# Gate and up products of a SwiGLU layer by seven block products instead of eight, with the down projection between them

## The chip, the cores and the metric

The kernel runs on one core of a Trainium2 chip. The metric is the device time of one execution in microseconds (us); lower is better. Engines are named as in the profile: PE is TensorE (PEld its weight loads), DVE VectorE, ACT ScalarE, POOL GpSimd, SP SyncE, whose queue issues the transfers.

## What is computed

A trunk of two layers on 512 tokens of width 1024: each layer is an attention (stick-breaking in the first, dilated windows in the second), then a SwiGLU of width 2816, each after an RMS norm and added to the residual stream; a last norm gives the output. All data is float32. The part that matters here:

```python
def _rmsnorm(h, g):
    hf = h.astype(jnp.float32)
    y = hf * lax.rsqrt(jnp.mean(hf * hf, axis=-1, keepdims=True) + NORM_EPS)
    return (y * g.astype(jnp.float32)).astype(h.dtype)

def _swiglu(h, w_gate, w_up, w_down):
    return (jax.nn.silu(h @ w_gate) * (h @ w_up)) @ w_down

    h = h + _swiglu(_rmsnorm(h, norm_ffn[layer]), w_gate[layer], w_up[layer], w_down[layer])
```

## The kernel before

**Data.** The residual stream H lies transposed on chip: 8 chunks of 128 model columns on the partitions, 512 tokens along the free dimension. A float32 product is made from float32r operands in three matmuls: each operand is split into a high part (rounded by a copy on ScalarE) and a low part (the difference, by VectorE), and high x high, high x low and low x high are added up in PSUM (`mm3`, L290). X holds both parts of the normed stream without its factor 1/rms; that factor, a row R of 512 tokens, is applied to the products.

**Weights.** The class `Weights` (L150) streams them in the order of their use as units of 128 x 512. `load` (L175) issues one transfer on SP's queue into one of 8 raw buffers; `split` (L186) makes the high part `whi` on ScalarE (L214) and the low part `wlo` on VectorE (L215); `get` (L220) hands out a unit and has those up to three units ahead split.

**Feed-forward layer** (`ffn`, L739). 22 chunks of 128 hidden columns. For a chunk, `gu` (L743) fills two PSUM banks, gate and up, with 8 x 3 matmuls of 512 columns each, from two weight units per bank; then VectorE scales the gate by R (L758), ScalarE applies SiLU (L759), GpSimd multiplies by R again (L762), VectorE multiplies by the up bank (L763), and the result is split into VO (L767, L768). `down` (L771) multiplies a part of the chunks (PARTS: 6, 6, 6 and 4 chunks) by the down weights for each of 8 output columns and adds the bank to H (`residual`, L651). `ffn_order` (L43) puts each part two chunks behind its last `gu`. `rstd_row` (L366) makes R from the sums of squares while chunk 0 is computed. In layer 1 the last part is `finish` (L798): it goes over the first half of the tokens for all outputs and then over the second, so that half the output can be normed and stored beside the other's products; its matmuls have 256 columns, and its weights stay on chip (`khi`, `klo`).

**Order.** The code writes instructions in the order of the lists above. The framework that builds the program then sets each engine's queue itself: it tracks which buffer each instruction reads and writes, adds the waits, and may put an instruction that is ready ahead of an earlier one that is not. Within a queue the instructions then start in that order. PSUM has 8 banks: three `z`, two `t`, two `pj`, one `av`.

```python
 23  PARTS = [(0, 6), (6, 12), (12, 18), (18, 22)]
290      def mm3(out, wh, wl, xh, xl, start, stop):
291          mm(out, wh, xh, start, False)
292          mm(out, wh, xl, False, False)
293          mm(out, wl, xh, False, stop)
651      def residual(n, p, e=slice(0, 512)):
652          dve.tensor_add(H[:, n, e], H[:, n, e], p[:, e])
```

Of the kernel before, what the change touches and what calls it, by code (L numbers as in the profile page):

```python
# [7 lines left out]
F = mybir.dt.float32  # L8
# [23 lines left out]
# Chunks of the output per transfer, and those that GpSimd scales, for both halves of the tokens.  # L32
# [9 lines left out]

def ffn_order():  # L43
    seq = []
    done = 0
    for i, (a, b) in enumerate(PARTS):
        upto = min(b + 2, NF) if i + 1 < len(PARTS) else NF
        for f in range(done, upto):
            seq.append(("gu", f))
        done = upto  # L50
        seq.append(("dn", i))
# [9 lines left out]
def raw_list():  # L61
    """Weight tiles in the order of their use: each holds two units."""
    raws = []
    for layer in range(2):
        raws += [(kind, layer, i) for kind, i in mixer_order()]
        for kind, i in ffn_order():
            if kind == "gu":
                raws.append(("gu", layer, i))
            else:
                raws += [("dn", layer, i, n) for n in range(0, 8, 2)]  # L70
    return raws


def raw_width(r):
    if r[0] == "dn":
        a, b = PARTS[r[2]]
        return 2 * 128 * (b - a)
    return 2048


def pack_weights(w_qkv_a, w_o_a, w_kv, w_q_b, w_o_b, w_gate, w_up, w_down):
    """The weights in the order of their use, each tile in the layout that it has on chip."""
# [4 lines left out]
    def block(m, r):  # L87
        return m[:, 256 * r[2]:256 * r[2] + 256].reshape(8, 128, 256).transpose(1, 0, 2).reshape(128, -1)
# [6 lines left out]
    for r in raw_list():  # L95
        l = r[1]
        if r[0] == "qk":
            t = cross(r, [cols(wq[l], r[2]), cols(wk[l], r[2])])
        elif r[0] == "v":
            t = [block(wv[l], r)]  # L100
        elif r[0] == "o":
            b = [block(wo[l], (0, 0, g)) for g in range(4)]
            t = [b[g][:, 512 * q:512 * q + 512] for g, q in O_ORDER[4 * r[2]:4 * r[2] + 4]]
        elif r[0] == "gu":
            t = cross(r, [cols(w_gate[l], r[2]), cols(w_up[l], r[2])])
        else:
            a, b = PARTS[r[2]]
            m = w_down[l][128 * a:128 * b]
            t = cross(r, [cols(m, r[3]), cols(m, r[3] + 1)])
        parts.append(np.concatenate(t, axis=1).reshape(-1))  # L110
# [3 lines left out]
def held(r):  # L114
    """The last part of the last layer's weights stays on chip for both halves of the tokens."""
    return r[0] == "dn" and r[1] == 1 and r[2] == len(PARTS) - 1


def crossed(r):
    """Whether the two units of a tile are used half by half in turn."""  # L120
    return r[0] in ("qk", "gu") and r[2] == 0 or (
        r[0] == "dn" and r[2] == len(PARTS) - 1 and r[3] == 0 and not held(r))


def cross(r, t):
    h = t[0].shape[1] // 2
    return [t[0][:, :h], t[1][:, :h], t[0][:, h:], t[1][:, h:]] if crossed(r) else t
# [22 lines left out]
class Weights:  # L150
    """Streams the weight tiles in and splits each quarter of them into its two float32r parts."""

    RAW = 8
    AHEAD = 3

    def __init__(self, tc, pool, wflat, gains):
        self.tc, self.nc, self.pool, self.w, self.gains = tc, tc.nc, pool, wflat, gains
        self.raws = raw_list()
        self.units = []
        for i, r in enumerate(self.raws):  # L160
            n = raw_width(r)
            for j in range(4):
                gain = None
                if r[1] == 1 and r[0] == "qk":
                    which, part = (j % 2, j // 2) if crossed(r) else (j // 2, j % 2)
                    gain = ("k", (G_MIX1, G_KV)[which] + 4 * part)
                elif r[1] == 1 and r[0] == "v":
                    gain = ("v", G_KV + 2 * j)
                self.units.append((i, j * n // 4, n // 4, gain))
        self.offs = np.concatenate([[0], np.cumsum([128 * raw_width(r) for r in self.raws])]).tolist()  # L170
        self.rt = {}
        self.wt = {}
        self.nload = self.nsplit = self.nget = 0

    def load(self):  # L175
        u = self.nload
        if u >= len(self.units):
            return
        i, o, n, _ = self.units[u]
        t = self.pool.tile([128, 512], F, name="raw", bufs=self.RAW)  # L180
# [5 lines left out]
    def split(self):  # L186
# [3 lines left out]
        while self.nload <= u:  # L190
            self.load()
# [37 lines left out]
def trunk(ctx, tc, xg, wflat, cst_d, cs_d, outT):  # L229
# [509 lines left out]
    def ffn(layer, slot0, done):  # L739
# [3 lines left out]
        def gu(f):  # L743
# [10 lines left out]
            if f == 0:  # L754
                rstd_row(pjbank)
# [132 lines left out]
```

## Time and profile before

| | us |
|---|---|
| three runs, median (lowest to highest) | 1257.61 (1257.53 to 1260.98) |
| span of the profiled execution | 1260.1 |
| its PE, DVE, ACT, POOL busy | 1237.6, 777.0, 594.5, 159.1 |
| attention of layer 1 (618.40 to 856.00) | 237.60 |
| feed-forward of layer 0 (247.05 to 618.40) | 371.35 |
| feed-forward of layer 1 up to the last part (856.00 to 1226.00) | 370.00 |

The profile page gives one execution; its span is the time from its first to its last instruction, and no separate time of that execution is given beside it. A row of the timeline has the start and the length of one instruction (or, with x2, of a merged run of them), its engine, its line, and the tiles as output<-inputs; brackets give idle time before it and what ended it. All products have line 288, that of a helper, so they are told apart by their tiles: z and t are banks of gate and up products, pj of the down projection, VO<-s the split hidden chunk.

### The profile page before, as it was taken

The page shows a single profiled execution, that of the slowest core. Times are in us where ns is not written, and L with a number is a line of the kernel's source. Part 1 is how long each engine was busy: PE and PEld are TensorE (multiplying, and loading weights), DVE is VectorE, ACT ScalarE, POOL GpSimd, SP SyncE. Part 2 cuts the span into 40 slices and gives each one's busy share as a digit, 9 for nine tenths or more (in the row PEclk, how much of TensorE's full clock was granted, in tenths as well). Part 3 has the DMA queues.
Part 4 walks back from the last instruction along what each step waited for, and adds up shares of the span by engine and source line. Part 5 has one row for each costly group of instructions (what it writes and reads, how often), then busy time and mean ns, then how long its engine had stood idle before and what let it go on. Part 6 is the DMA issues. An engine that isn't in the chain of part 4 may idle for free.

```text
span 1260.1 us, 17566 instructions
## 1 busy us (share of the span) xinstructions
PE 1237.6 (98%) x6041; PEld 1024.2 (81%) x6041; DVE 777.0 (62%) x1457; ACT 594.5 (47%) x1160; POOL 159.1 (13%) x237
## 2 busy tenths in 40 slices
PE   9999999999999999999899999999999999999997
PEld 7888988888888888888688788887888888888887
DVE  6799899873444443444868898788734444444455
ACT  6667666543323323323457676766533233233243
POOL 0000000011001101000434343100110011010001
PEclk9999999999999999999999999999999999999999
DMA  7743543233232233231445556551332332332321
GB/s 255 175 139 113 148 138 101 66 100 91 77 119 92 69 115 99 76 102 55 122 132 135 143 139 164 133 144 56 104 92 77 116 93 70 115 99 75 102 76 68
DMA packets 78953, 138.09 MB, mean 110 GB/s; under 512 B 10128, under 2 KB 28560, under 8 KB 78864
## 3 DMA queue, kind: packets, MB, share of 16 engines
q1 hardware_dynamic: 78864, 136.97, 37.5%
q8 instruction: 48, 0.79, 0.3%
q14 instruction: 41, 0.34, 0.1%
HBM read 106.00 MB, written 2.10 MB: 86 GB/s over the span
## 4 chain that ended last, share of the span: by engine, by line
PE 92%; DVE 3%; DMA 2%; issue 1%; ACT 1%; POOL 0%; SPq 0%; POOLq 0%; DVEq 0%
PE pj L288 40%; PE z L288 29%; PE t L288 17%; PE av L288 3%; PE t L604 2%; DMA rp<-rp 1%; DVE wlo L215 1%; DMA mov<-hl 1%; DMA H<-xg 0%; POOL H L822 0%; DVE H L652 0%; DVE z L582 0%; DMA raw<-wflat 0%; DVE al L611 0%; DVE VO L528 0%
## 5 line engine op out<-in xcount | busy, mean ns | idle before, releaser
L214 ACT ACTIVATE whi<-raw 128x512 fp32r<-128x512 f32 (+2 forms) x416 | 247.9, 598 | 476.8 <-PE pj L288 193.0
L215 DVE TENSOR_TENSOR wlo<-raw,whi 128x512 fp32r<-128x512 f32 (+2 forms) x416 | 280.0, 675 | 196.5 <-ACT whi L214 195.7
L288 PE MATMUL z<-X,whi 128*128 128x512 f32 x848 | 269.6, 396 | 0.0
L288 PE MATMUL pj<-VO,whi 128*128 128x512 f32 x832 | 264.2, 398 | 1.2 <-DVE H L652 1.1
L288 PEld LDWEIGHTS z<-X,whi 128*128 128x128 f32 x848 | 159.7, 188 | 38.9
L288 PEld LDWEIGHTS pj<-VO,whi 128*128 128x128 f32 x832 | 154.9, 188 | 39.2 <-issue 1.5
L288 PE MATMUL t<-X,whi 128*128 128x512 f32 x560 | 178.8, 396 | 0.0
L288 PE MATMUL pj<-X,whi 128*128 128x512 f32 x512 | 166.2, 404 | 4.3 <-DVE H L652 3.1
L288 PE MATMUL z<-X,wlo 128*128 128x512 f32 x424 | 168.1, 396 | 0.0
L288 PE MATMUL pj<-VO,wlo 128*128 128x512 f32 x416 | 164.9, 396 | 0.0
L762 POOL TENSOR_TENSOR s<-s,R 128x512 f32<-128x512 f32 x44 | 56.7, 1290 | 655.6 <-ACT s L759 634.0
L288 PEld LDWEIGHTS t<-X,whi 128*128 128x128 f32 x560 | 105.5, 188 | 25.7
L288 PEld LDWEIGHTS pj<-X,whi 128*128 128x128 f32 x512 | 93.6, 190 | 26.2 <-issue 3.9
L288 PE MATMUL t<-X,wlo 128*128 128x512 f32 x280 | 111.0, 396 | 0.0
L288 PE MATMUL pj<-X,wlo 128*128 128x512 f32 x256 | 102.2, 399 | 0.2 <-DVE wlo L215 0.2
L288 PEld LDWEIGHTS z<-X,wlo 128*128 128x128 f32 x424 | 79.9, 188 | 19.5
L652 DVE TENSOR_TENSOR H<-H,pj 128x512 f32<-128x512 f32 (+1 forms) x88 | 57.5, 659 | 59.1 <-PE pj L288 58.8
L288 PEld LDWEIGHTS pj<-VO,wlo 128*128 128x128 f32 x416 | 78.3, 188 | 18.9
L288 PE MATMUL pj<-whi,X 128*128 128x256 f32 x384 | 75.3, 286 | 1.3 <-DVE rp L459 1.3
L203 POOL TENSOR_TENSOR raw<-raw,H 128x512 f32<-128x512 f32 x48 | 55.4, 1162 | 65.6 <-DMA raw<-wflat 59.6
L288 PEld LDWEIGHTS pj<-whi,X 128*128 128x128 f32 x384 | 61.6, 190 | 2.0 <-DVE rp L459 1.6
L288 PEld LDWEIGHTS t<-X,wlo 128*128 128x128 f32 x280 | 52.7, 188 | 12.9
(149 smaller groups left out, 1606.6 us busy)
## 6 DMA issues: line engine op xcount, KB each, us to landing
raw<-wflat SPq DMA_DIRECT2D x304, 256.0 KB, 3.0
raw<-wflat SPq DMA_DIRECT2D x96, 192.0 KB, 2.3
mov<-hl SPq DMA_DIRECT2D x64, 256.0 KB, 4.3
sta<-hl SPq DMA_DIRECT2D x64, 128.0 KB, 2.4
raw<-wflat SPq DMA_DIRECT2D x32, 128.0 KB, 2.2
rp<-rp SPq DMA_DIRECT2D x56, 64.0 KB, 2.2
H<-xg SPq DMA_DIRECT2D x7, 256.0 KB, 5.6
outT<-H SPq DMA_DIRECT2D x2, 512.0 KB, 4.9
```

The source lines that it names most:

```text
L203: nc.gpsimd.tensor_mul(v3, v3, g.unsqueeze(2).to_broadcast([128, n // m, m]))
L214: nc.scalar.activation(hi[:, :n], v, AF.Copy)
L215: nc.vector.tensor_sub(lo[:, :n], v, hi[:, :n].bitcast(F))
L288: pe.matmul(out, a, b, start=start, stop=stop, skip_group_check=True)
L604: pe.transpose(b[:, o:o + 128], pr[i][:, 128 * c:128 * c + 128], idf)
L652: dve.tensor_add(H[:, n, e], H[:, n, e], p[:, e])
L762: pool.tensor_mul(t, t, R)
```

## The change

Chunks 0 and 1 of each layer stay as they were. The other 20 go in ten pairs g = 1 to 10. For a pair, the weights W (two chunks; gate and up are the two block rows, the halves of the 1024 model columns the two block columns) and the normed stream B (halves of the model columns by halves of the tokens) are blocks of a 2 x 2 product, and Strassen's scheme in the form with 15 additions gives the four results from seven block products, P1 to P7. A product has 256 tokens: per chunk 4 x 3 matmuls of 256 columns. Four of B's combinations are made once per layer (`token_sums`, into XT, beside chunk 1), from copies of H scaled by the gain. Four of the weights' combinations are made for each chunk in `split`. P6 and P7 add up in P1's bank, P3 in P5's, and copies of the banks between them give the partial sums. The scaling, SiLU, multiplication and splitting follow for both chunks of a half of the tokens at once, put off by steps (`after`, `stepped`). The down projection is cut into parts of 2, 4, 4, 4, 4 and 4 chunks; BESIDE says behind which product of which pair its steps (one output column of one part) stand. Raw weights have 16 buffers, split weights seven, and `get` keeps up to six units ahead. Layer 1's last weights go into X's memory.

```diff
-PARTS = [(0, 6), (6, 12), (12, 18), (18, 22)]
+PARTS = [(0, 2), (2, 6), (6, 10), (10, 14), (14, 18), (18, 22)]
...
+PRODUCTS = ("P1", "P2", "P6", "P5", "P7", "P4", "P3")
+BESIDE = {1: {4: (0, 3), 5: (0, 3), 6: (0, 2)}, 3: {3: (1, 1), 4: (1, 1), 5: (1, 1), 6: (1, 1)},
+          4: {0: (1, 1), 2: (1, 1), 4: (1, 1), 6: (1, 1)}, 5: {3: (2, 1), 4: (2, 1), 5: (2, 1), 6: (2, 1)},
+          6: {0: (2, 1), 2: (2, 1), 4: (2, 1), 6: (2, 1)}, 7: {3: (3, 1), 4: (3, 1), 5: (3, 1), 6: (3, 1)},
+          8: {0: (3, 1), 2: (3, 1), 4: (3, 1), 6: (3, 1)}, 9: {3: (4, 1), 5: (4, 1)},
+          10: {0: (4, 1), 3: (4, 1), 5: (4, 1)}}
...
+    for g in range(1, NF // 2):
+        for i, p in enumerate(PRODUCTS):
+            seq.append(("pr", g, p))
+            out(*BESIDE.get(g, {}).get(i, (0, 0)))
+    for part in range(len(PARTS)):
...
+                for i in range(2):
+                    f = 2 * step[1] + i
+                    w = lambda r, c: unit(("w", layer, f, r, c), 512)
+                    what = {"P1": lambda: ("raw", w(0, 0)), "P2": lambda: ("raw", w(0, 1)),
+                            "P6": lambda: ("s2", w(1, 0), w(1, 1), w(0, 0)), "P5": lambda: ("s1",),
+                            "P7": lambda: ("s3", w(1, 0), w(0, 0)), "P4": lambda: ("raw", w(1, 1)),
+                            "P3": lambda: ("s4", w(0, 1))}[step[2]]()
...
-    RAW = 8
-    AHEAD = 3
+    RAW, RAW2 = 8, 8
+    W, W2 = 4, 3
+    AHEAD = {"mix": 3, "ffn": 6, "held": 6}
...
+        if what[0] == "raw":
+            v = r[0]
+        elif what[0] == "s2":
+            s1, s2 = (self.pools["sum"].tile([128, 512], F, name="sum", bufs=4) for _ in range(2))
+            nc.vector.tensor_add(s1, r[0], r[1])
+            nc.vector.tensor_add(s2, s1, r[2])
+            self.sums[what[-1]] = (s1, s2)
+            v = s2
+        elif what[0] == "s1":
+            v = self.sums[what[-1]][0]
+        elif what[0] == "s3":
+            nc.vector.tensor_add(r[0], r[0], r[1])
+            v = r[0]
         else:
+            v = self.sums.pop(what[-1])[1]
+            nc.vector.tensor_add(v, v, r[0])
...
+        def token_sums(p, XT):
+            B = p.tile([128, 8, 512], F, name="B")
+            t = [p.tile([128, 4, 256], F, name=f"tk{i}") for i in range(2)]
+            b12, b21, b22 = B[:, 0:4, 256:512], B[:, 4:8, 0:256], B[:, 4:8, 256:512]
+            b11 = B[:, 0:4, 0:256]
+            def block(c):
+                g = gains[:, (G_FFN0, G_FFN1)[layer] + c:(G_FFN0, G_FFN1)[layer] + c + 1]
+                act.activation(B[:, c, :], H[:, c, :], AF.Copy, scale=g)
+            def high(i, v):
+                act.activation(XT[:, i, 0], v, AF.Copy)
+            def low(i, v):
+                dve.tensor_sub(XT[:, i, 1], v, XT[:, i, 0].bitcast(F))
+            def first():
+                dve.tensor_sub(t[0], b11, b12)
+                high(1, t[0])
+            def second():
+                dve.scalar_tensor_tensor(t[1], t[0], -1.0, b22, op0=OP.mult, op1=OP.subtract)
+                high(0, t[1])
+            def third():
+                dve.tensor_sub(t[1], b22, b12)
+                high(2, t[1])
+            def fourth():
+                dve.tensor_add(t[0], b21, t[1])
+                high(3, t[0])
+            for c in range(8):
+                block(c)
+            return [first, second, lambda: low(1, t[0]), lambda: low(0, t[1]), fourth, third,
+                    lambda: low(3, t[0]), lambda: low(2, t[1])]
...
+            return {"P1": plain(0, 0), "P2": plain(4, 0), "P3": plain(4, 1), "P6": summed(0),
+                    "P5": summed(1), "P7": summed(2), "P4": summed(3)}[p]
...
+        def product(g, p, XT):
+            new = {"P1": ("a", zb), "P2": ("b", tb), "P5": ("e", zb), "P4": ("c", tb)}.get(p)
+            if new:
+                st[new[0]] = new[1]()
+            name = {"P1": "a", "P6": "a", "P7": "a", "P2": "b", "P5": "e", "P3": "e", "P4": "c"}[p]
+            bank = st[name]
+            x = moving(p, XT)
+            for i in range(2):
+                wh, wl = W.get("pr")
+                out = bank[:, 256 * i:256 * i + 256]
+                for c in range(4):
+                    w = slice(128 * c, 128 * c + 128)
+                    mm(out, wh[:, w], x(c, 0), bool(new) and i == 0 and c == 0, False)
+                    mm(out, wh[:, w], x(c, 1), False, False)
+                    mm(out, wl[:, w], x(c, 0), False, c == 3)
+                if i == 0:
+                    stepped()
+            if p == "P1":
+                st["g", 0] = TS()
+                act.activation(st["g", 0], a, AF.Copy)
+            elif p == "P2":
+                dve.tensor_add(st["g", 0], st["g", 0], b)
+                after(2, lambda t=st["g", 0]: dve.tensor_mul(
+                    t.rearrange("p (f n) -> p f n", f=2), t.rearrange("p (f n) -> p f n", f=2),
+                    R[:, 0:256].unsqueeze(1).to_broadcast([128, 2, 256])))
+                after(3, lambda t=st["g", 0]: act.activation(t, t, AF.Silu))
+            elif p == "P6":
+                st["g", 1] = TS()
+                act.activation(st["g", 1], a, AF.Copy)
+            elif p == "P7":
+                st["u", 0], st["u", 1] = (W.pools["w2"].tile([128, 512], F, name="up", bufs=2) for _ in range(2))
+                act.activation(st["u", 0], a, AF.Copy, scale=-1.0)
+                dve.tensor_sub(st["u", 1], st["u", 0], e)
+            elif p == "P4":
+                dve.tensor_add(st["u", 0], st["u", 0], c)
+                _, _, scaled_up, prod, high, low = gated(0, f0)
+                scaled_up()
+                after(3, prod)
+                after(4, high)
+                after(5, low)
+            elif p == "P3":
+                dve.tensor_add(st["g", 1], st["g", 1], e)
+                scaled_gate, silu, scaled_up, prod, high, low = gated(1, f0)
+                scaled_up()
+                scaled_gate()
+                after(1, silu)
+                after(2, prod)
+                after(3, high)
+                after(4, low)
...
+        def down(part, n):
+            a, b = PARTS[part]
             m = b - a
+            wh, wl = W.get("dn")
+            p = pjbank()
+            for k in range(m):
+                c = slice(128 * k, 128 * k + 128)
+                g = gs[a + k]
+                mm3(p, wh[:, c], wl[:, c], g[:, 0:512], g[:, 512:1024], k == 0, k == m - 1)
+            residual(n, p)
+            stepped()
+            if part == len(PARTS) - 1:
+                done(n)
+            elif m == 4:
+                stepped()
...
+        with tc.tile_pool(name=f"ff{layer}", bufs=1, reuse_waits="tile") as fp:
+            XT = fp.tile([128, 4, 2, 4, 256], FR, name="XT")
+            W.pools["w2"] = fp
+            gu(0)
+            with tc.tile_pool(name=f"tk{layer}", bufs=1, reuse_waits="tile") as tp:
+                gu(1, token_sums(tp, XT))
+            with tc.tile_pool(name=f"wr{layer}", bufs=1, reuse_waits="tile") as wp:
+                W.pools["raw2"] = W.pools["sum"] = wp
+                W.loads()
+                for step in order[2:]:
+                    if step[0] == "pr":
+                        product(*step[1:], XT)
+                    elif layer == 1 and step[1] == len(PARTS) - 1:
+                        break
+                    else:
+                        down(*step[1:])
...
+    W.kept = X
```

## Rows read from the trace of the kernel before

**Rows 1.** The page: busy us, share and instructions of each engine; span in 40 slices

```profile
span 1260.1 us, 17566 instructions
PE 1237.6 (98%) x6041; PEld 1024.2 (81%) x6041; DVE 777.0 (62%) x1457; ACT 594.5 (47%) x1160; POOL 159.1 (13%) x237
PEclk9999999999999999999999999999999999999999
```

**Rows 2.** The page: chain that ended last, shares of the span by engine

```profile
PE 92%; DVE 3%; DMA 2%; issue 1%; ACT 1%; POOL 0%; SPq 0%; POOLq 0%; DVEq 0%
```

**Rows 3.** Windows: feed-forward layer 0, attention layer 1, feed-forward layer 1, tail

```profile
core 0: us, PE busy (x) PEld busy (x) DVE busy (x) ACT busy (x) POOL busy (x), PEclk, DMA share, GB/s
247.05:618.40 371.35, 370.25 (x1581) 297.41 (x1580) 174.76 (x273) 127.65 (x218) 37.69 (x30) 1.00 0.31 93
618.40:856.00 237.60, 226.43 (x1285) 195.42 (x1284) 195.47 (x478) 157.69 (x357) 73.00 (x87) 0.99 0.52 138
856.00:1226.00 370.00, 370.00 (x1588) 296.99 (x1587) 177.31 (x286) 133.83 (x233) 29.39 (x23) 1.00 0.31 91
1226.00:1260.10 34.10, 25.90 (x213) 25.07 (x211) 18.13 (x49) 11.03 (x26) 6.15 (x9) 0.93 0.18 63
```

**Rows 4.** Timeline of PE, tail, first and 25th matmul; window of the tail's first half

```profile
1228.96 0.28 PE L288 MATMUL t<-VO,khi 128*128 128x256 f32 x1
...
1231.80 0.28 PE L288 MATMUL pj<-VO,khi 128*128 128x256 f32 x1
...
1226.00:1240.30 14.30, 14.30 (x121) 14.22 (x120) 7.64 (x17) 5.60 (x12) 1.23 (x2) 1.00 0.01 2
```

**Rows 5.** Timelines of DVE and ACT: operations back to back (start us, us)

```profile
275.80 0.68 DVE L215 TENSOR_TENSOR wlo<-raw,whi 128x512 fp32r<-128x512 f32 x1
276.41 1.29 DVE L768 TENSOR_TENSOR VO<-s,VO 128x512 fp32r<-128x512 f32 x2
...
1201.22 0.42 DVE L215 TENSOR_TENSOR klo<-raw,khi 128x256 fp32r<-128x256 f32 x1 [0.45 <-ACT khi L214]
1207.55 1.09 DVE L215 TENSOR_TENSOR klo<-raw,khi 128x256 fp32r<-128x256 f32 x3
...
1206.27 0.63 ACT L214 ACTIVATE whi<-raw 128x512 fp32r<-128x512 f32 x1 [0.91 <-PE z L288]
1206.81 0.40 ACT L214 ACTIVATE khi<-raw 128x256 fp32r<-128x256 f32 x1
```

**Rows 6.** Timeline at 279.4 us: GpSimd's multiplication and VectorE beside it

```profile
279.64 1.28 POOL L762 TENSOR_TENSOR s<-s,R 128x512 f32<-128x512 f32 x1 [4.47 <-ACT s L759]
280.12 1.35 DVE L215 TENSOR_TENSOR wlo<-raw,whi 128x512 fp32r<-128x512 f32 x1 [1.22 <-ACT whi L214]
```

**Rows 7.** Timelines of DVE and ACT from 255 us, start of feed-forward layer 0

```profile
258.93 0.69 DVE L215 TENSOR_TENSOR wlo<-raw,whi 128x512 fp32r<-128x512 f32 x1 [2.94 <-ACT whi L214]
261.39 3.35 DVE L379 RECIPROCAL s<-s 128x512 f32<-128x512 f32 x1 [0.57 <-ACT s L378]
264.66 0.63 DVE L215 TENSOR_TENSOR wlo<-raw,whi 128x512 fp32r<-128x512 f32 x1
...
267.86 0.69 DVE L215 TENSOR_TENSOR wlo<-raw,whi 128x512 fp32r<-128x512 f32 x1 [0.77 <-ACT whi L214]
269.19 0.69 DVE L758 TENSOR_TENSOR s<-t,R 128x512 f32<-128x512 f32 x1
...
264.34 0.63 ACT L214 ACTIVATE whi<-raw 128x512 fp32r<-128x512 f32 x1 [2.18 <-PE z L288]
```

**Rows 8.** Waits: who waited for whom, us in total, times, longest

```profile
DVE wlo L215 <- ACT whi L214: 195.7, 151, 2.9
ACT whi L214 <- PE pj L288: 193.0, 156, 4.5
```

More of the change, by code (lines that the diff above doesn't have):

```diff
@@ L150 @@
 class Weights:
-    RAW = 8
-    AHEAD = 3
+    RAW, RAW2 = 8, 8
+    W, W2 = 4, 3
+    AHEAD = {"mix": 3, "ffn": 6, "held": 6}
     def __init__(self, tc, pool, wflat, gains):
         self.tc, self.nc, self.pool, self.w, self.gains = tc, tc.nc, pool, wflat, gains
[L158 to L172, printed above, removed]
+        self.units, self.ops = weight_stream()
+        self.offs = np.concatenate([[0], np.cumsum([128 * n for _, n in self.units])]).tolist()
+        last = {}
+        for n, op in enumerate(self.ops):
+            for u in self.used(op):
+                last[u] = n
+        self.ends = {}
+        for u, n in last.items():
+            self.ends.setdefault(n, []).append(u)
+        first = {}
+        for n, op in enumerate(self.ops):
+            for u in self.used(op):
+                first.setdefault(u, n)
+        self.uring, self.oring = [], []
+        q = 0
+        for u in range(len(self.units)):
+            ffn = self.ops[first[u]][1] == "ffn"
+            self.uring.append("raw2" if ffn and q % 16 >= 8 else "raw")
+            q = q + 1 if ffn else 0
+        q = 0
+        for op in self.ops:
+            ffn = op[1] == "ffn"
+            self.oring.append("held" if op[1] == "held" else "w2" if ffn and q % 7 >= 4 else "w")
+            q = q + 1 if ffn else 0
+        self.last_product = max(n for n, op in enumerate(self.ops) if op[0] == "pr")
+        self.size = {"raw": self.RAW, "raw2": self.RAW2, "w": self.W, "w2": self.W2, "held": 8}
+        self.live = dict.fromkeys(self.size, 0)
+        self.pools = {"raw": pool, "w": pool}
+        self.rt, self.wt, self.sums = {}, {}, {}
@@ L186, in split, with ready @@
+    def ready(self, u, now):
+        _, zone, what, _ = self.ops[u]
+        ring = self.oring[u]
+        if self.live[ring] >= self.size[ring] or (ring == "w2" and ring not in self.pools):
+            return False
+        if what[0] == "s2" and "sum" not in self.pools:
+            return False
+        if zone == "held" and now <= self.last_product:
+            return False
+        return all(v < self.nload or self.uring[v] in self.pools for v in self.used(self.ops[u]))
     def split(self):
@@ L844, in finish @@
             scaled_out(1)
-        for kind, i in ffn_order():
-            (gu if kind == "gu" else down)(i)
+        order = ffn_order()
+        with tc.tile_pool(name=f"ff{layer}", bufs=1, reuse_waits="tile") as fp:
[12 more added lines that the diff above has]
+                        break
+                    else:
+                        down(*step[1:])
+                while later:
+                    stepped()
+                for k in ("raw2", "sum", "w2"):
+                    del W.pools[k]
+        if layer == 1:
+            a, b = PARTS[-1]
+            finish(a, b - a)
+    W.kept = X
+    W.kept0 = next(u for u, (key, _) in enumerate(W.units) if key[:3] == ("dn", 1, len(PARTS) - 1))
     for c in range(8):
```

266 lines of the change are left out of this document (154 added, 112 removed).

## The prediction

> **What bounds the kernel now.** I read the page's summary first: TensorE is busy for 98% of the span at the full clock, VectorE for 62%, ScalarE for 47% [rows 1]. The chain that ended last says the same: 92% of it is TensorE [rows 2]. So removed matmul time comes off the end, if nothing else takes its place. The stages [rows 3] say where: the two feed-forward layers take 371.35 and 370.00 us (the second without its last part, which is the tail), and TensorE idles for about 1 us in the first and not at all in the second. VectorE is busy for 174.76 of the 371.35 us there, ScalarE for 127.65. The profiled execution's span is 1260.1 us; the three runs have a median of 1257.61, so the span lies 2.5 us (0.2%) above it. The sum is made on the trace and taken off the median.
>
> **What is removed and added on TensorE.** A feed-forward layer before has 22 chunks of gate and up (48 matmuls of 512 columns each) and 22 x 8 x 3 of the down projection: 1584, in 371.35 us, so 0.2344 us each. A pair of chunks costs 96 x 0.2344 = 22.50 us. After the change, ten pairs per layer use 7 products x 2 chunks x 4 blocks x 3 = 168 matmuls of 256 columns. The same shape (split weights stationary, 256 columns of tokens moving) runs in the tail: 24 of them start between 1228.96 and 1231.80, 0.1183 us each, and 120 in a stretch of 14.30 us, 0.119 [rows 4]. I take 0.1185: 168 x 0.1185 = 19.91 us. A pair gains 2.59 us, twenty pairs **51.9 us**. The point where the gain is nothing is 22.50 / 168 = 133.9 ns a matmul. The down projection has the same matmuls before and after, in another order; chunks 0 and 1 stay as they were. A layer's TensorE time becomes 371.35 - 25.9 = 345.4 us.
>
> The Trainium skill, "TensorE: Matmul & The Clock Gate", section "Back-to-back issue gap", speaks against this change: it gives sustained spacings of about 131 ns at 512 columns and 81 ns at 128, which drawn as a line is an estimate of 98 ns at 256, well over half of 131; by that a pair would go from 12.6 to 16.4 us. The rows of this trace, 234 and 118.5 ns, do not agree with it, and the sum goes by the rows.
>
> **What is added on VectorE and ScalarE.** Two VectorE operations of 128x512 back to back take 1.29 us where one takes 0.69, so each further one costs 0.60; on ScalarE the next one starts 0.54 after the last [rows 5]. VectorE per pair before: 8 low parts of weights and 6 operations of the two chunks, 14 x 0.60 = 8.4 us. After: 14 low parts (seven products, two chunks), 8 additions of weights (two for P6, one each for P7 and P3, twice), and 10 at the products' ends (add of P2, P7, P4, P3, two scalings by R, two products, two low parts) = 32 x 0.60 = 19.3 us. GpSimd's two multiplications per pair stay, but now they meet a busy VectorE: the one operation caught under a GpSimd one took 1.35 instead of 0.69 [rows 6], so 2 x 0.66 more: 20.6 us. ScalarE: 21 x 0.54 = 11.3 us, never the bound. A down step of four chunks adds 0.60 for its weights and 0.60 for its addition to the residual stream, beside 12 x 0.2344 = 2.81 us of TensorE; one of two chunks 0.60 + 0.34 (three low parts of 256 columns take 1.09, one 0.42 [rows 5]) beside 1.41.
>
> The Trainium skill, "SBUF — State Buffer", section "Who interferes with whom", says that the pair of ports shared by VectorE and GpSimd is locked for a whole instruction, not shared; at that, both 1.28 us would count in full, 21.9 instead of 20.6 us a pair. The one caught here began 0.48 us after GpSimd's and lost 0.66, which agrees in kind; it would take some 1.3 us more from pair 2 of each layer.
>
> TensorE against VectorE, pair by pair: pair 1 (eight small down steps) 31.2 against 20.6 + 7.5 = 28.1; pair 2 (none) 19.9 against **20.6**; pairs 3 to 8 (four steps each) 31.2 against 25.4; pair 9 (two) 25.5 against 23.0; pair 10 (three) 28.3 against 24.2. So VectorE fits, with nothing to spare in pair 2. Its cover is TensorE's own time; where that is gone, TensorE waits for weights or for a PSUM bank.
>
> **The start of each layer is where it does not fit.** Between the start of chunk 1 and the end of pair 2 TensorE needs 11.25 + 31.2 + 19.9 = 62.3 us. VectorE in that time must do the row of 1/rms (0.60 + 3.3 for the reciprocal + 3 x 0.60 = 5.7 us), 4 low parts of chunk 1's weights (2.4; both in [rows 7]), the ends of chunks 0 and 1 (6 x 0.60 + 1.3 = 4.9), and the new token sums: 4 sums and 4 low parts of 1024 elements. The trace has no such size; twice a 512-element step is 1.2 us, between 1.2 and 2 x 0.69 = 1.4; I take 1.2, as one instruction cannot cost more than two. That is 9.6 us, and with pairs 1 and 2 (28.1 + 20.6) 71.3 us: 9.0 too much. VectorE's idle 2.94 us ahead of chunk 1 [rows 7] can take some, which leaves 6.1; if TensorE can run one product (2.84 us) ahead of it, 3.3; if the weights' lead of six units (10 operations, 6.0 us) must be kept full as well, 12.1. I take **7 us per layer**. ScalarE's eight scaled copies of the residual stream and four high parts (8 x 0.54 + 4 x 1.1 = 8.7 us) fall in gaps of over 2 us that it has there [rows 7].
>
> Other edits, with one answer each: the loads bring the same bytes from the same queue into 16 buffers instead of 8, at a DMA share of 0.31 [rows 3], so nothing, and at most one load's landing at a layer's start; nothing is moved past another queue's work on SP. The residual additions rise from 32 to 48 per layer, inside the count above. P6 and P7 add onto P1's bank, P3 onto P5's, so each must wait until ScalarE or VectorE has read it; one product, 2.84 us, lies between, which hides a read of 0.69. The kept weights of the last part move into X's memory and wait for the last product; 8.4 us of down steps lie between. For all of these and the ends of the layers I take 2 us per layer, between 0 and 4.
>
> **Sum:** 51.9 - 2 x 7 - 2 x 2 = 33.9; 1257.6 - 33.9 = **1223.7 us**. A feed-forward layer then takes about 354 us.
>
> **The rivals.**
> (a) All of it is hidden. TensorE stays full and the gain is 48 to 52 us: 1206 to 1210. For it: VectorE was idle for half of these stages, and low parts of weights stand in the queue ahead of chunk 0's scaling, which the code writes first [rows 7], so ready work is put ahead of waiting work. Against it: the 9 us of the start.
> (b) VectorE becomes the bound. Six of a pair's 14 weight units are sums made by VectorE, turned by ScalarE and taken back by VectorE; if nothing is put between, each costs a round trip of 0.63 and two hand-overs, about 0.79 us (VectorE stood 0.77 us for ScalarE's high part of a weight at 267.86 [rows 7]; there are 151 such waits, 195.7 us [rows 8]). Then a pair has 25.3 us: pair 1 loses 1.7, pair 2 5.4, pair 9 2.2, pair 10 0.6, and the start 12.1: 22 per layer, 44 in all, **1250 us**. Pairs 3 to 8 still fit (30.1 against 31.2).
> (c) Slower: the shared PSUM banks. P6, P7 and P3 of each pair, 60 places, start only when the bank they add to has been read. If each read queues behind work that waits for something else, and one product of cover is not enough, TensorE stands at all of them. It decides at 51.9 / 60 = 0.87 us a place. With a read of ScalarE and one of VectorE in the open, 0.63 + 0.69 = 1.32 us, it costs 79 us: **1285 us**. For it: ScalarE's high parts wait for TensorE in hundreds of places, 193.0 us in the largest group [rows 8], so its queue does stand. Against it: a wait for a buffer to come free ends within half a product, well inside the cover.
> (d) The change does not do what it says: a 256-column matmul with the new operands costs more than in the tail. Weight loads are busy for 14.22 of 14.30 us there [rows 4], so the margin is thin. Each 10 ns costs 33.6 us; a quarter more, 148 ns, gives 20 x (24.9 - 22.5) = 47 us more than before, 1305. The spacings of the Trainium skill's section "Back-to-back issue gap", named above, would be this case. Against it: 120 matmuls of this very shape at 119 ns.
>
> **How the numbers follow.** My forecast (VectorE late at each start, else hidden; 1213 to 1237) 0.55; (a) and its surroundings down to 1206 0.13; (b), 1237 to 1254, 0.17; (c) 0.10; (d) 0.05. A measurement can tell about 0.3% (3.8 us). Faster: 0.55 + 0.13 + 0.15 of (b) = 0.83; same 0.05, from the edges of (b) and (c); slower 0.12. The range 1207 to 1252 holds the forecast, nearly all of (a) and (b), about 0.83, and leaves out the slower cases.
>
> **What would show it.** Right: matmuls of 256 columns 118 to 120 ns apart inside pairs 3 to 8 with no gaps; about 1440 more matmul records; VectorE busy for some 80% of a feed-forward layer; TensorE's new idle time between chunk 1 and pair 3, ended by VectorE's sums or low parts. Wrong: gaps at P6, P7 and P3 in every pair, ended by the reads of the banks (c); gaps of 5 us in pair 2 and VectorE never idle there (b); a longer spacing without any gaps (d); or a layer of 345 to 347 us (a).

## The result, and the profile after

The changed kernel takes 1218.97 us (median of four runs, 1217.75 to 1220.04) where the kernel before takes 1257.57 beside it: a ratio of 0.969, with a 95% interval of 0.9668 to 0.9712. That is 38.6 us less, far beyond the spread of executions (1253.22 to 1260.98 us for the kernel before); 33.9 us less had been forecast.

First the page of the changed kernel: busy time of each engine, and the shares of the chain that ended last.

```profile
span 1216.0 us, 21067 instructions
PE 1187.4 (98%) x7481; PEld 1060.8 (87%) x7481; DVE 1021.9 (84%) x1833; ACT 698.8 (57%) x1332; POOL 173.2 (14%) x237
...
PE 85%; DVE 6%; DMA 3%; ACT 2%; issue 2%; POOL 1%; SPq 0%; POOLq 0%; DVEq 0%; ACTq 0%
```

Against [rows 1] TensorE has 1440 more matmuls (7481 for 6041), as forecast, and 50.2 us less busy time (1187.4 for 1237.6); VectorE has 376 more operations and 244.9 us more. The chain [rows 2] has gone from 92% to 85% TensorE, and VectorE's share has doubled from 3% to 6%: somewhere TensorE now waits for VectorE. Which stage that is, the windows say (columns as in [rows 3]: TensorE, weight loads, VectorE, ScalarE, GpSimd, granted clock, DMA share, GB/s; feed-forward layer 0, attention layer 1, feed-forward layer 1, tail):

```profile
247.25:601.16 353.91, 347.52 (x2307) 316.78 (x2306) 304.42 (x466) 179.37 (x303) 50.12 (x35) 1.00 0.34 101
601.16:848.64 247.48, 242.36 (x1373) 208.09 (x1372) 202.63 (x503) 171.06 (x384) 70.41 (x85) 1.00 0.50 131
848.64:1181.40 332.76, 327.04 (x2212) 301.51 (x2211) 286.05 (x445) 171.32 (x289) 33.96 (x22) 0.99 0.34 98
1181.40:1216.00 34.60, 26.06 (x213) 25.31 (x211) 17.57 (x48) 10.40 (x25) 6.16 (x9) 0.90 0.18 62
```

TensorE idles for 6.39 us of the first layer (353.91 less 347.52) and 5.72 of the second; before it was 1.10 and 0.00 by the cuts of [rows 3]. VectorE is busy for 304.42 of 353.91 us, 86%. To subtract stages, the same cuts must be used on both traces, from the first gate matmul of a layer to the first matmul of the next mixer. The cuts of [rows 3] are others: 856.00 lies in the attention, 20.9 us ahead of layer 1's first gate matmul (876.92), so the 370.00 us called a feed-forward layer there hold that much attention; and 618.40 lies ahead of layer 0's last down products. Cut alike, feed-forward layer 0 goes from 373.85 to 353.91 us (19.9 less), feed-forward layer 1 with the tail from 383.2 to 367.3 (15.8 less), and the attention layer between them from 256.0 to 247.5, though no step of the change lies in it. Each trace is one execution: these two differ by 44.1 us in span, the medians by 38.6. The traced execution of the kernel before is a long one (1260.1 us, where 26 later ones have spans of 1252.1 to 1258.7). More of that attention stage below.

The idle time isn't spread out. The same columns, for the first 78 us of layer 0 and then for most of the pairs 3 to 10 of both layers:

```profile
258.60:270.20 11.60, 11.60 (x51) 9.33 (x50) 11.60 (x13) 6.63 (x9) 0.00 (x0) 1.00 0.17 47
270.20:275.30 5.10, 2.11 (x15) 1.67 (x13) 5.09 (x7) 3.49 (x4) 1.46 (x1) 1.00 0.62 171
275.30:285.00 9.70, 7.00 (x50) 6.20 (x50) 9.15 (x14) 5.65 (x10) 1.81 (x2) 1.00 0.14 45
...
330.00:440.00 110.00, 110.00 (x766) 102.19 (x765) 92.22 (x147) 53.52 (x92) 8.78 (x7) 1.00 0.37 107
...
917.00:1150.00 233.00, 233.00 (x1655) 218.13 (x1655) 196.15 (x312) 114.17 (x194) 24.84 (x16) 1.00 0.36 100
```

Between 270.20 and 285.00 TensorE is busy for 9.11 of 14.80 us and VectorE for 14.24; in the middle of the layers TensorE has no gap at all in 343 us, with VectorE busy for 84% of it. So what the page averages over the span is one short stretch per layer where VectorE is the bound, and a long one where it is not. The timeline of TensorE shows what the stretch waits for (start, us, operation; in brackets the idle time and what ended it). P1 and P6 write a z bank, P2 a t bank, and here P2 has started ahead of P1; XT holds the token sums, w2hi and w2lo are the parts of a weight in the second set of split buffers:

```profile
270.23 0.39 PE L388 MATMUL t<-X,whi 128*128 128x256 f32 x2
271.87 0.38 PE L388 MATMUL t<-X,wlo 128*128 128x256 f32 x1 [1.25 <-DVE wlo L307]
...
273.16 0.40 PE L388 MATMUL t<-X,whi 128*128 128x256 f32 x2
275.34 0.50 PE L388 MATMUL z<-X,whi 128*128 128x256 f32 x2 [1.78 <-DVE s L875]
...
279.32 0.28 PE L388 MATMUL t<-X,wlo 128*128 128x256 f32 x1
281.60 0.51 PE L388 MATMUL z<-XT,w2hi 128*128 128x256 f32 x2 [2.00 <-ACT w2hi L306]
282.74 0.38 PE L388 MATMUL z<-XT,w2lo 128*128 128x256 f32 x1 [0.64 <-DVE w2lo L307]
```

Of each gap, the part above the usual distance from one start to the next (0.119 us after 256 columns) counts: 1.41, 1.95, 2.16 and 0.80 us, with 0.35 in pair 1's down steps 6.7 us in layer 0; in layer 1, by the same count, 3.27, 1.72, 0.81 and 0.36, 6.2 us. The timeline of VectorE tells why:

```profile
269.39 1.22 DVE L910 TENSOR_TENSOR tk<-B 128x1024 f32<-128x1024 f32 x1
270.53 0.68 DVE L482 SCALAR_TENSOR_TENSOR R<-s 128x512 f32<-128x512 f32 x1
271.13 0.68 DVE L307 TENSOR_TENSOR wlo<-raw,whi 128x512 fp32r<-128x512 f32 x1
271.74 0.68 DVE L875 TENSOR_TENSOR s<-t,R 128x512 f32<-128x512 f32 x1
272.33 2.35 DVE L899 TENSOR_TENSOR XT<-tk,XT 128x1024 fp32r<-128x1024 f32 x2
274.60 0.68 DVE L875 TENSOR_TENSOR s<-z,R 128x512 f32<-128x512 f32 x1
...
280.20 0.68 DVE L281 TENSOR_TENSOR sum<-sum,raw 128x512 f32<-128x512 f32 x1
```

The low part that P2 needs (at 271.13) stands behind a token sum of 1.22 us. Then P1 needs a PSUM bank that a plain chunk still holds until VectorE has scaled it by R (L875), and that scaling, at 274.60, stands behind two low parts of the token sums, 2.35 us, though R itself is there at 271.2. The gap before the first P6 ends with the weight sum: a sum of VectorE (280.20), then its high part on ScalarE. It is one queue that is full, not one slow operation.

Two more readings answer to the kernel before. The waits (who waited for whom; us, times, longest) answer to [rows 8]: 195.7 us of VectorE's waiting for high parts have become 38.7 (25.8, and 12.9 in the second set of buffers). At the 0.79 us that rival (b) charged to each of 120 weight sums it would be 95 us, so that round trip is for the most part not paid.

```profile
DVE wlo L307 <- ACT whi L306: 25.8, 45, 3.6
...
DVE w2lo L307 <- ACT w2hi L306: 12.9, 21, 0.7
```

And the end of feed-forward layer 0, in TensorE's timeline, first of the kernel before and then of the changed one:

```profile
617.06 0.70 PE L288 MATMUL pj<-VO,whi 128*128 128x512 f32 x2 [1.09 <-DVE H L652]
620.90 0.47 PE L288 MATMUL pj<-X,whi 128*128 128x512 f32 x1 [0.80 <-DVE H L652]
```

```profile
603.76 0.47 PE L388 MATMUL pj<-X,whi 128*128 128x512 f32 x1 [1.51 <-DVE H L752]
```

Before, the last down projection (617.06) and the first matmul of the next layer (620.90) each waited for VectorE's additions to the residual stream. Above the usual spacing they are 1.26 and 0.96 us. After, both waits are gone, but for 0.55 us between two down steps; what is left at 603.76 has its like before (2.32 us at 625.56), 0.8 us longer.

### The profile page after: what moved, and what is told of

The parts are those of the page before. It is cut to its first block, busy times and chain, and to the rows that moved or that the text cites. A ratio compares the mean times of both kernels' runs of the same rounds, so it can differ in the third digit from the quotient of the medians.

```text
span 1216.0 us, 21067 instructions
## 1 busy us (share of the span) xinstructions
PE 1187.4 (98%) x7481; PEld 1060.8 (87%) x7481; DVE 1021.9 (84%) x1833; ACT 698.8 (57%) x1332; POOL 173.2 (14%) x237
## 4 chain that ended last, share of the span: by engine, by line
PE 85%; DVE 6%; DMA 3%; ACT 2%; issue 2%; POOL 1%; SPq 0%; POOLq 0%; DVEq 0%; ACTq 0%
PE pj L388 38%; PE z L388 30%; PE t L388 11%; PE av L388 3%; PE t L704 3%; DMA mov<-hl 1%; DVE wlo L307 1%; DVE H L752 1%; DMA raw<-wflat 1%; DMA rp<-rp 0%; DMA H<-xg 0%; DVE sum L280 0%; DVE w2lo L307 0%; DVE X L422 0%; DVE sum L281 0%
## 5 line engine op out<-in xcount | busy, mean ns | idle before, releaser
L306 ACT ACTIVATE whi<-raw 128x512 fp32r<-128x512 f32 (+1 forms) x290 | 178.2, 620 | 139.1 <-PE pj L388 50.2
L307 DVE TENSOR_TENSOR wlo<-raw,whi 128x512 fp32r<-128x512 f32 (+1 forms) x290 | 203.4, 709 | 25.0 <-ACT whi L306 22.6
L388 PE MATMUL pj<-VO,whi 128*128 128x512 f32 x568 | 180.7, 398 | 0.5 <-DVE H L752 0.4
L388 PE MATMUL z<-XT,whi 128*128 128x256 f32 x560 | 99.7, 280 | 0.0
L388 PE MATMUL z<-X,whi 128*128 128x256 f32 (+1 forms) x464 | 96.4, 301 | 1.8 <-DVE s L875 1.8
L388 PEld LDWEIGHTS z<-XT,whi 128*128 128x128 f32 x560 | 86.2, 189 | 0.7
L388 PE MATMUL pj<-VO,w2hi 128*128 128x512 f32 x264 | 83.1, 396 | 0.4 <-ACT VO L957 0.4
L388 PEld LDWEIGHTS z<-X,whi 128*128 128x128 f32 x464 | 75.1, 189 | 7.0 <-DVE s L875 2.0
L307 DVE TENSOR_TENSOR w2lo<-raw,w2hi 128x512 fp32r<-128x512 f32 (+1 forms) x102 | 70.1, 688 | 11.8 <-ACT w2hi L306 11.5
L388 PE MATMUL z<-XT,wlo 128*128 128x256 f32 x280 | 78.5, 280 | 0.0
L388 PE MATMUL z<-XT,w2hi 128*128 128x256 f32 x400 | 74.9, 287 | 3.6 <-ACT w2hi L306 3.6
## 6 DMA issues: line engine op xcount, KB each, us to landing
raw<-wflat SPq DMA_DIRECT2D x384, 256.0 KB, 2.8
mov<-hl SPq DMA_DIRECT2D x64, 256.0 KB, 4.5
H<-xg SPq DMA_DIRECT2D x7, 256.0 KB, 5.4
```

What stands on the lines that cost most here:

```text
L306: nc.scalar.activation(hi[:, :n], v, AF.Copy)
L307: nc.vector.tensor_sub(lo[:, :n], v, hi[:, :n].bitcast(F))
L388: pe.matmul(out, a, b, start=start, stop=stop, skip_group_check=True)
```

## The experiments

The theory: TensorE's time falls by 51.9 us, and only the start of each layer gives some back, since VectorE has more work there than fits. Against it stood the forecast's rivals, a VectorE that is the bound throughout (b), waits at the shared banks (c), a dearer matmul (d), and a further one: that the new order of the down projection makes a part of the gain.

**The order alone.** The changed kernel with all its down steps in their new places, but every pair done as two plain chunks, without products or sums.

```diff
     for g in range(1, NF // 2):
-        for i, p in enumerate(PRODUCTS):
-            seq.append(("pr", g, p))
-            out(*BESIDE.get(g, {}).get(i, (0, 0)))
+        for j in range(2):
+            seq.append(("gu", 2 * g + j))
+            for i in ((0, 1, 2, 3), (4, 5, 6))[j]:
+                out(*BESIDE.get(g, {}).get(i, (0, 0)))
...
```

> The new order of the down projection and its smaller parts, with all 22 chunks as eight products of 512 columns. Theory (the gain is the saved matmul time): the same as the kernel before, 1257.6 us within 4, a feed-forward layer of 371 to 374 us, no waits at a layer's start. Rival (the placing of the down steps gives part of the gain by itself): 1250 us or less.

Measured: 1254.14 us (12 runs), ratio 0.9976 (0.9965 to 0.9986). That is 3.0 us less, within the 4 of the theory and short of the rival's 1250, but the interval leaves out a ratio of 1. Its stages say where: layer 0 takes 371.49 us for 373.85, layer 1 with the tail 383.6 for 383.2. These 2.4 us are nearly all the waits at the end of layer 0 (1.26 and 0.96 us), which are gone here too; the next one, at the first products of the attention, is 0.8 us shorter (1.63 us above the usual spacing for 2.47). The kernel keeps the 16 raw buffers and the lead of six units as well, so what these bring is in the 3.0; the places speak for the order. It is a small part of 38.6, and it had not been in the forecast.

**Halves without the products.** The kernel before, with each gate and up matmul of chunks 1 to 21 cut into two of 256 columns: 2016 more matmuls, the same columns, nothing else.

```diff
-                        mm3(p, wh[:, c], wl[:, c], X[:, k, 0, :], X[:, k, 1, :], k == 0, k == 7)
+                        for e in range(2):
+                            x = slice(256 * e, 256 * e + 256)
+                            mm3(p[:, x], wh[:, c], wl[:, c], X[:, k, 0, x], X[:, k, 1, x], k == 0 and e == 0, k == 7)
```

> The kernel before with gate and up of chunks 1 to 21 in two halves of the tokens: 2016 matmuls of 512 columns become 4032 of 256, nothing else. Theory (0.119 us each, as in the changed kernel's pairs): 2016 x (2 x 0.119 - 0.2344) = 7.3 us more, 1262 to 1267. Rival (the cost does not halve, the spacing is 130 ns or more when this shape runs for long): 2016 x 0.0256 = 52 us more, 1309 or above.

Measured: 1265.47 us, ratio 1.0065 (1.0046 to 1.0084), 8.3 us more, as the theory has it. Spread over 4032 matmuls that is 2.1 ns each on top of half of 234.4: 119.3 ns. Rival (d) falls. Its layer 0 in the windows, and two points of TensorE's timeline, with eight matmuls between their starts in 0.96 us:

```profile
248.80:625.80 377.00, 375.05 (x2595) 347.82 (x2593) 176.77 (x276) 128.60 (x220) 37.99 (x31) 1.00 0.31 93
```

```profile
299.81 0.28 PE L288 MATMUL z<-X,whi 128*128 128x256 f32 x1
...
300.77 0.28 PE L288 MATMUL t<-X,whi 128*128 128x256 f32 x1
```

The spacings that the Trainium skill gives in "TensorE: Matmul & The Clock Gate", section "Back-to-back issue gap" (131 ns at 512 columns, 81 at 128) disagree with this kernel, where 512 columns take 234 ns and 256 take 118 to 120. By the estimate of 98 ns drawn from them the halves would have cost 2016 x (2 x 98 - 131) = 131 us; they cost 8.3.

**Without the token sums.** The changed kernel with the eight VectorE operations per layer of the token sums left out.

```diff
             def first():
-                dve.tensor_sub(t[0], b11, b12)
-                high(1, t[0])
+                high(1, b12)
...
             def low(i, v):
-                dve.tensor_sub(XT[:, i, 1], v, XT[:, i, 0].bitcast(F))
+                pool.memset(XT[:, i, 1].bitcast(F), 0.0)
```

> The changed kernel without the token sums' eight VectorE operations of 1024 elements per layer (9.6 us each layer): XT's high parts are plain copies of blocks, its low parts zeros written by GpSimd, so the sums are left out. Theory (VectorE has more work at the start than TensorE has time): the waits of 6.7 and 6.2 us between chunk 1 and pair 2 fall below 2 us each, 1208 to 1211 us. Rival (the first product waits for a bank that chunk 0 or 1 holds until the row R of 1/rms is there, whatever else VectorE does): a wait of 3 us or more per layer stays, 1213 to 1217.

Measured: 1209.91 us (ratio 0.9626, 0.9605 to 0.9646), 9.1 less than the changed kernel by the medians, 8.0 by the ratios. The time is in the range of the theory. The waits for a low part and for the scaling by R are gone from the start, and with them the rival, so the late scaling was the token sums' doing. What stays is the first P6's weight sum, 2.09 us in layer 0 and 1.07 and 1.18 in layer 1, and with a wait among the down steps (0.41 and 0.36) it is 2.5 and 2.6 us, more than the 2 that were expected:

```profile
277.03 1.03 PE L388 MATMUL z<-XT,w2hi 128*128 128x256 f32 x4 [1.93 <-ACT w2hi L306]
```

**Without the weight sums.** The same for the eight additions of weights per pair: the products take the first weight of their sum.

```diff
-            nc.vector.tensor_add(s1, r[0], r[1])
-            nc.vector.tensor_add(s2, s1, r[2])
...
-            nc.vector.tensor_add(r[0], r[0], r[1])
+        else:
             v = r[0]
-        else:
-            v = self.sums.pop(what[-1])[1]
-            nc.vector.tensor_add(v, v, r[0])
...
```

> The changed kernel without the eight additions of weights per pair: the split units are the plain blocks, so the combinations of weights are left out; 8 x 0.60 = 4.8 us less VectorE work in every pair. Theory (VectorE is late at the start alone): the wait for the first P6 (2.2 + 0.8 us in layer 0) goes, the earlier ones stay, and pairs 3 to 10 gain nothing: 1209 to 1215 us. Rival (VectorE sets the pace of all pairs): 20 us or more, below 1199.

Measured: 1212.16 us (0.964, 0.9627 to 0.9653), 6.8 less, although 160 operations and some 90 us of VectorE's time went (1021.9 to 932.5 us busy). Rival (b), in which VectorE's sums set the time throughout, falls: the steady pairs give nothing back because they had lost nothing. In layer 0 the wait of the first P6 is gone and the two ahead of it stay, in TensorE's timeline; in layer 1 (last line) the first P6 waits after all, 3.08 us above the usual spacing:

```profile
271.02 0.38 PE L376 MATMUL t<-X,wlo 128*128 128x256 f32 x1 [1.26 <-DVE wlo L295]
274.49 0.52 PE L376 MATMUL z<-X,whi 128*128 128x256 f32 x2 [1.79 <-DVE s L863]
...
876.37 0.50 PE L376 MATMUL z<-XT,w2hi 128*128 128x256 f32 x2 [2.92 <-ACT s L974]
```

That wait is another one: P6 comes before P2 there and waits for P1's copy by ScalarE (L974), which ends at 876.32, the mechanism of rival (c). P2 could hardly have gone ahead of it, since the scaling that frees its bank ends at 876.17, behind two low parts of the token sums; so it is the start's overload once more. A second wait for P1's copy, 0.58 us, stands in pair 3 of that layer.

These two experiments take away different parts of one queue, and each leaves waits of the other. Their gains are not to be added, since less work in the queue also moves what stands behind it.

**More VectorE work in the middle.** If VectorE fits in pairs 3 to 8 with time to spare, further work should be hidden there. Eight additions of 128x512 per pair, whose result nothing uses:

```diff
+            if 3 <= g <= 8 and p in ("P1", "P6", "P7", "P4"):
+                for _ in range(2):
+                    dve.tensor_add(ACC, CS[:, 0, :], CS[:, 1, :])
```

> The changed kernel with eight additions of 128x512 more on VectorE in each of pairs 3 to 8 of both layers: 12 x 8 x 0.60 = 57.6 us of work that nobody reads. Theory (TensorE sets the pace there, VectorE has 31.2 - 25.4 = 5.8 us to spare per pair and 4.8 are added): 1219 to 1224 us. Rival (VectorE is at the edge there): 40 us or more longer, 1259 or above.

Measured: 1230.74 us (0.9787, 0.9766 to 0.9808), 11.8 more than the changed kernel for 57.6 us of work. Both expectations miss: the cover holds most of it, not all. Two of the new gaps, in TensorE's timeline, and ScalarE's operation that ends the first:

```profile
397.73 0.28 PE L388 MATMUL t<-X,w2lo 128*128 128x256 f32 x1
399.36 0.51 PE L388 MATMUL z<-XT,w2hi 128*128 128x256 f32 x2 [1.35 <-ACT s L989]
...
464.04 0.50 PE L388 MATMUL z<-XT,whi 128*128 128x256 f32 x2 [1.93 <-ACT s L989]
...
398.73 0.58 ACT L989 ACTIVATE s<-z 128x512 f32<-128x512 f32 x1
```

This too is the mechanism of rival (c): P6 adds onto P1's bank, and P1's copy (L989 in this kernel) stands in ScalarE's queue until 398.73. It comes at the first P6 of two pairs per layer (1.5 and 2.1 us in each, 7.2 in all), pairs 5 and 7. These have no down step ahead of the end of their fourth product; but pair 3 has none there either, and does not wait.

The profiled execution is 13.5 us longer than the changed kernel's, and most of the rest is a lower clock, told in the last section: about 5.5 us more lost to it, by the spacing of the matmuls. That part is not shown to come from the added work: three of its four stretches (at 272.8, 283.1 and 883.8 us) lie at a layer's start, ahead of pair 3. The one execution with a granted clock like the changed kernel's, 0.994, took 1227.73 us, 8.8 more than the changed kernel. So (c) is real and small: a load of 8 x 0.60 = 4.8 us more per pair, nearly all that VectorE has to spare (16% of some 31 us), brings it out at two of a layer's thirty places.

**Nine pairs.** If the start is where the loss lies, it should pay to give two chunks back to the plain form: it costs a pair's gain in each layer, 2 x 2.59 us, and puts 22.5 us of TensorE work between the token sums and the first product.

```diff
-    seq = [("gu", 0), ("gu", 1)]
+    seq = [("gu", 0), ("gu", 1), ("gu", 2), ("gu", 3)]
...
-    for g in range(1, NF // 2):
+    for g in range(2, NF // 2):
...
                 gu(1, token_sums(tp, XT))
+                gu(2)
+                gu(3)
...
```

The eight small down steps beside pair 1 move to pair 2.

> The changed kernel with chunks 2 and 3 as eight products of 512 columns too, so nine pairs instead of ten; the eight small down steps move from pair 1 to pair 2. It gives back 2.59 us of matmul time per layer, 5.2 in all, and gives VectorE 22.5 us in which chunks 2 and 3 ask for 8.4. Theory (the waits come from too much VectorE work at the start): the waits of 6.7 and 6.2 us fall below 1 us each, 1219 + 5.2 - 11 to 14 = 1210 to 1213 us, with the clock full throughout the start of layer 1. Rival (the first pair always waits, for its sums or for a bank, wherever it stands): 3 us or more per layer stay, 1217 or above.

Measured: 1208.94 us (0.9619, 0.9606 to 0.9633), 10 less than the changed kernel and the lowest median of all, 1 us under the range of the theory. Feed-forward layers 0 and 1 in its windows, the same columns:

```profile
246.60:595.00 348.40, 348.14 (x2235) 314.44 (x2234) 293.63 (x448) 174.59 (x294) 51.75 (x35) 1.00 0.36 103
844.90:1175.00 330.10, 328.69 (x2161) 298.86 (x2160) 274.83 (x429) 166.37 (x280) 35.08 (x22) 1.00 0.34 99
```

TensorE idles for 0.26 and 1.41 us in place of 6.39 and 5.72, with more matmul time to do. Layer 0's waits fall below the 1 us that was expected, layer 1's to 1.5, and the rival's 3 us are not there. The working: waits of 12.9 us become 1.8 (0.31, then 0.68 and 0.82), a clock loss of 2.7 us in layer 1 (last section) is gone, two pairs' gain of 5.2 is given up: 8.6 us, beside 10.0 by the medians and 8.9 by the ratios (0.969 and 0.9619 of 1257.5).

**Nine pairs, token sums spread** over chunks 1 and 2 rather than all beside chunk 1 (one per half of a chunk's weights in place of two).

> As e5_nine_pairs, and the steps of the token sums are written one behind each half bank of chunks 1 and 2, not two behind each of chunk 1. Theory: VectorE's work is the same and the queue is ordered by readiness, so the same as e5_nine_pairs within 2 us. Rival (the place in the code decides): a difference of 3 us or more, either way.

Measured: 1209.52 us (0.9617, 0.9604 to 0.963), the same as with nine pairs: once the start has room, where in it the sums stand makes no difference.

## Why the prediction was right

Its mechanism was the right one, and its sum came within 4.7 us, with a term of the wrong sign in it. By steps:

- **The pair's gain, 51.9 us.** Shown. Inside pairs the matmuls stand 118 to 120 ns apart (median 118), and the halves alone cost 119.3. Taken at 119 instead of 118.5 it is 0.8 us less per layer.
- **The start of each layer, 7 us.** Shown in place, cause and size: 6.7 and 6.2 us, ended by VectorE's low parts, its scaling and its sums, all of them before pair 1 is over, and nearly gone with nine pairs. That the size fits so well is in part luck: the working gave 6.1, 3.3 or 12.1 us by what is counted, and 7 was picked between them. One wait had been named only in general ("or for a PSUM bank"): P1 and P2 wait for banks of plain chunks until VectorE has scaled these by R. The new sums delay the scalings, so the wait is the same overload by another door. Pair 2, the tightest by the forecast, has no gap above 0.3 us.
- **Other seams, 2 us lost per layer.** Wrong in sign. No such loss is seen; instead the new order took away 1.7 us of waits at the end of layer 0 and 0.8 at the start of the attention behind it, and order and buffers without the products are worth 3.0 us. The working counted what could be added at the layers' ends and did not ask which waits of before stood there to be lost: one was in the 1.10 us of idle time of [rows 3], the other lay behind the cut at 618.40.
- **The rows.** The 370.00 us taken for a feed-forward layer begin in the attention, as said above. The sum does not rest on them. The spacing that it does rest on holds for the whole of layer 0 as well: 373.85 us less 2.2 of waits, over 1584 matmuls, is 0.2346.
- **The clock** was not in the sum: 2.7 us in layer 1.
- **VectorE per pair.** The forecast's 25.4 of 31.2 us in pairs 3 to 8 is 81%; the windows show 84%. Its 0.66 us for a meeting with GpSimd was too much: 0.15 in the mean (last section).

Together, on the two traces: layer 0 is 25.9 - 6.7 - 0.8 + 1.7 = 20.1 us (19.9 seen), layer 1 is 25.9 - 6.2 - 0.8 - 2.7 = 16.2 (15.8 seen). The other 8.5 us by which the traces differ lie in the attention layer. Of these, 0.8 are the shorter wait at its first products: 2.47 and 2.52 us above the usual spacing in the two profiles with the old order (before and halves), 1.58 to 1.94 in the seven with the new one. Another 2.8 are TensorE's clock, which fell twice in that stage of the traced execution of before (last section) and not in the changed kernel's. The rest are small waits that vary from profile to profile: the stage takes 256.0 us in the one profile of the kernel before, 251.3 with the halves, 247.5 to 252.4 in the others. Of the 38.6 us between the medians, the two layers and the shorter wait make 36.5; the 2 that are left were not tried by themselves and stay open.

The rivals: (a), all of it hidden, falls with layers of 353.91 us in place of 345 to 347 and the waits at the start. (b) falls with 343 us in the middle of the layers without a gap and with 90 us of VectorE work taken away for a gain of 6.8. (c) has no gap of its kind above 0.2 us in the changed kernel; its wait comes out at two places per layer once 4.8 us of further VectorE work are added to each pair, and at two in layer 1 without the weight sums. (d) falls with the halves.

## What to carry to other kernels

When work moves from a bound engine to a half-idle one, make the balance stretch by stretch: the average (84% busy) hid one stretch of 15 us where the second engine had more than it could do. Where a scheme needs preparation, keep some of the old, cheap-to-feed form at its start: two chunks per layer fewer in the new form cost 5 us and won back some 14. And before reordering, list the waits that stand at the old seams; some of the gain may be there.

## What the runs showed of the hardware

**TensorE's clock fell in the middle of the kernel.** At the start of layer 1, the windows of the changed kernel (columns as above, the granted clock is the third figure from the right):

```profile
874.00:878.00 4.00, 1.04 (x9) 0.84 (x8) 4.00 (x5) 3.42 (x4) 0.96 (x1) 1.00 0.56 170
878.00:882.00 4.00, 3.85 (x20) 3.88 (x21) 3.44 (x6) 1.89 (x3) 1.80 (x2) 0.57 0.29 92
882.00:886.00 4.00, 1.80 (x11) 1.40 (x10) 4.00 (x8) 1.86 (x3) 0.00 (x0) 0.87 0.03 8
886.00:890.00 4.00, 4.00 (x27) 4.00 (x26) 4.00 (x8) 1.79 (x4) 0.00 (x0) 0.70 0.45 124
```

and TensorE's timeline there:

```profile
874.76 0.28 PE L388 MATMUL z<-X,wlo 128*128 128x256 f32 x1
878.15 0.77 PE L388 MATMUL t<-X,whi 128*128 128x256 f32 x2 [3.11 <-DVE s L875]
878.72 0.42 PE L388 MATMUL t<-X,wlo 128*128 128x256 f32 x1
...
881.28 0.41 PE L388 MATMUL t<-X,wlo 128*128 128x256 f32 x1
```

From 878.72 to 881.28 twelve matmuls start in 2.56 us, 213 ns each: that is 256 columns at 1.2 GHz, the lower level. TensorE had stood for 3.27 us just before; after the next waits, 1.72 and 0.81 us, it runs slowly again until 888.4. The stretches from 878.15 to 881.49 and from 885.82 to 888.50 hold 15 and 13 matmuls and would have taken 1.78 and 1.54 us at 118.5 ns; they took 3.34 and 2.68: 2.7 us lost. In layer 0, waits of 1.41, 1.95 and 2.16 us left the clock at 1.00. Such a stretch follows waits at the start in the kernels without token sums and without weight sums and in the one with more VectorE work, and none is seen with nine pairs. The kernel before has two as well, in the attention of layer 1, behind waits of 2.32 us (at 625.56) and 2.05 us (at 766.94):

```profile
626.00:630.00 4.00, 4.00 (x13) 3.12 (x12) 2.79 (x3) 0.60 (x2) 1.48 (x2) 0.62 0.24 75
768.00:772.00 4.00, 4.00 (x26) 4.00 (x25) 3.79 (x16) 2.53 (x7) 2.69 (x5) 0.71 0.57 155
```

By the spacing they cost it 2.8 us. Its traced execution has a mean granted clock of 0.995, the lowest of all that are recorded of it (0.996 to 0.998 in 26 others); the four of the changed kernel have 0.992 to 0.995, which speaks for such a loss in each of them. So a wait of some microseconds is paid for twice where the clock then falls, and a forecast of waits should carry that as a bound.

**GpSimd waits for VectorE, more than the other way.** In the kernel with spread token sums, one GpSimd multiplication and VectorE beside it:

```profile
889.48 5.22 POOL L876 TENSOR_TENSOR s<-s,R 128x512 f32<-128x512 f32 x1 [4.48 <-ACT s L875]
```

```profile
889.25 0.69 DVE L307 TENSOR_TENSOR w2lo<-sum,w2hi 128x512 fp32r<-128x512 f32 x1
889.86 0.68 DVE L281 TENSOR_TENSOR sum<-sum,raw 128x512 f32<-128x512 f32 x1
...
892.87 0.69 DVE L287 TENSOR_TENSOR raw<-raw 128x512 f32<-128x512 f32 x1
894.73 0.69 DVE L877 TENSOR_TENSOR s<-s,t 128x512 f32<-128x512 f32 x1 [1.18 <-POOL s L876]
```

It takes 5.22 us where [rows 6] has 1.28, and ends 1.14 us after VectorE's last operation (893.56), which is nearly the time it needs alone: it looks as if it did not begin its work until VectorE stopped, while VectorE kept its pace of 0.60. The same is seen in layer 0 of that kernel, 5.16 us at 290.35. The forecast's 0.66 us that VectorE pays at each meeting is one side only. In the changed kernel GpSimd's product with R takes 1.57 us in the mean of 40. Over its 44 such multiplications in the feed-forward layers GpSimd takes 11.9 us more than 1.29 each, and VectorE's operations beside them 6.8 us more than alone, 0.15 a meeting. VectorE's 112 additions of 128x512 to H, with an operand in PSUM, take 0.69 us at most, those beside GpSimd too. The Trainium skill, "SBUF — State Buffer", section "Who interferes with whom", has the rule that whichever engine issues first holds the shared ports and the other is blocked; these rows and [rows 6], where GpSimd came first, agree with it. That the blocked one stands behind seven instructions in a row is seen in these rows alone.
